# Dilated attention: keeping the queries in three token orders, copied by ScalarE one branch ahead

## The chip, the core and the metric

One core of a Trainium2 chip runs the whole program: TensorE (PE, matmuls and weight loads), VectorE (DVE), ScalarE (ACT), GpSimd (POOL) and SyncE (SP), which issues nearly all DMAs. The metric is device time of one launch, in microseconds (us); lower is better.

## The reference, cut to what matters

The layer is a bidirectional encoder block over two requests, 256 prompt tokens and 2,048 sample tokens (2,304 rows in all), with a Hyena half (long convolutions by FFT) and an attention half beside it, then an output projection and a gated MLP. The change lies in the attention half: 8 heads of 64, three dilated sliding-window branches, merged by their softmax denominators.

```
DILATED_BRANCHES = ((128, 1), (512, 4), (2048, 16))

def dilated_branch(q, k, v, slopes, window, dilation):
    ...
    R = window // (2 * dilation)          # 64 in every branch
    Ls = T // dilation
    ...
    def by_residue(a):                    # token t belongs to residue t % dilation
        return a.reshape(B, Ls, dilation, H, E).transpose(0, 2, 1, 3, 4)
    ...
    s = jnp.einsum('brnqhe,brnkhe->brnhqk', qb, kb).astype(jnp.float32) * (E ** -0.5)
    ...                                   # ALiBi bias, |rel| <= R, softmax
```

In the branch of dilation 4 a query attends to keys at distance 4, 8, ... up to 256 tokens; in that of dilation 16 to keys at 16, 32, ... tokens.

## The kernel before, in words

Queries and keys lie in DRAM head by head, transposed (`d_qT`, `d_kT`: 64 rows a head, 2,304 tokens along the free axis). `prepare` (line 851) brings one head into SBUF in four chunks of 576 tokens, each twice, on partitions 0 to 63 and 64 to 127: ScalarE rounds the queries to `Qh` (line 862), VectorE leaves the rest in `Ql` (the helper `sub`, line 201), ScalarE and GpSimd make the upper half of `Ks` the rest of the keys (line 865 and line 201), VectorE rounds the lower half (line 867). So one fp32 product is two fp32r matmuls: `Qh` and then `Ql` are the stationary operands, `Ks` streams (lines 902 and 903).

`attention` goes over four pairs of heads (hp 0 to 3), in each over three branches (b 0, 1, 2 for dilations 1, 4, 16), in each over 18 blocks of 128 queries, 216 blocks in all. For the sample, branches 0 and 1 have `win` blocks: 128 queries against a window of 192 keys at the ends of a residue and of 256 elsewhere. In branch 0 the prompt adds two such blocks; in branch 1 a residue has four blocks (192, 256, 256, 192 keys). Branch 2 has one `res` block a residue (two residues of 128 keys are streamed, 256 columns). In branches 1 and 2 the prompt is two `pack` blocks (every second token). Queries and keys both lie in natural order, so their slices step by 1, 4 or 16 tokens, by 2 in `pack` blocks:

```
t0 = off + res + dil * P * j
qs = slice(t0, t0 + dil * (P - 1) + 1, dil)
...
rhs = Ks[:, m0:m0 + dil * (n - 1) + 1:dil]
```

A block goes through these steps: four weight loads and matmuls into the scores `aS`, two of each a head (`scores`); VectorE adds the bias and takes the minimum (line 906); ScalarE takes the exponential into `aP` and its sum (line 909); `flip` transposes `aP` on TensorE into `aT` (line 918), and ScalarE, or VectorE for every third block, copies it to `aPT` (lines 922 and 925); `values` multiplies by the values into `aOp` (line 933); for every group of up to four blocks ScalarE copies `aOp` to `aOC` (line 938), TensorE transposes it (`aOT`, line 946), VectorE writes `aO` and a DMA stores it. `aS` and `aT` have two buffers each, `aOp` one. Every engine works its own instructions in order.

The Hyena half of the sample runs beside the attention, woven in by `weave` at fixed rates (90 to 440): `hs2z`, `hs2k`, `hs` matmuls, DVE products, ScalarE copies `hbe` and `hae` (lines 742 and 692). After the generators have given a program order, a scheduler sets the order on each engine from modelled durations; what is ready early moves forward.

The six tiles of a head pair (`Ql`, `Ks`, `Qh` for two heads) are allocated a head pair ahead, and `prepare` of the next pair is stepped once in six blocks (`if k % 6 == 0: next(ahead, None)`). When head pair 3 begins, the pool of the first head's tiles closes (`mq.close()`), and the pool for the start of the output projection takes its place; three weight tiles `ow` take over buffers of the tag `qk` (line 1044).

Of the kernel before, what the change touches and what calls it, by code (L numbers as in the profile page):

```python
# [13 lines left out]
F32 = mybir.dt.float32  # L14
F32R = mybir.dt.float32r
# [6 lines left out]
P = 128  # L22
D = 1024
NT = 2304
LP, LS = 256, 2048
# [162 lines left out]
class Hybrid:  # L188
# [662 lines left out]
    def prepare(self, head, tiles):  # L851

        nc = self.nc
        Ql, Ks, Qh = tiles
        up = slice(64, 128)
        hr = slice(64 * head, 64 * head + 64)
        for c0 in range(0, NT, 576):
            cc = slice(c0, c0 + 576)
            for t, src in ((Ql, self.qT), (Ks, self.kT)):
                for d in range(2):  # L860
                    nc.sync.dma_start(out=t[64 * d:64 * d + 64, cc].bitcast(F32), in_=src[hr, cc])
            nc.scalar.copy(Qh[:, cc], Ql[:, cc].bitcast(F32))
            self.sub(nc.vector, Ql[:, cc], Ql[:, cc].bitcast(F32), Qh[:, cc])
            kh = self.qkp.tile([P, 576], F32R, tag="kh", name="kh", bufs=1)
            nc.scalar.copy(kh[up], Ks[up, cc].bitcast(F32))
            self.sub(nc.gpsimd, Ks[up, cc], Ks[up, cc].bitcast(F32), kh[up])
            nc.vector.tensor_copy(Ks[0:64, cc], Ks[0:64, cc].bitcast(F32))
            yield

    def attention(self, wp, psS, psT, psO, first, mq):  # L870
        nc, a = self.nc, self.a
        q1, q2, q3 = [], [], []

        def scores(heads, g, i, blk, ot, bias, b):
            r, kind, _ = g
# [5 lines left out]
            for hh in range(2):  # L881
                Ql, Ks, Qh = heads[hh]
                t0 = off + res + dil * P * j
                qs = slice(t0, t0 + dil * (P - 1) + 1, dil)
                if kind == "win":
                    qa, qb = Qh[:, qs], Ql[:, qs]
                    k0 = max(0, P * j - 64)
                    n = min(nb * P, P * j + 192) - k0
                    v0, N = 0, n
                    b0 = k0 - (P * j - 64)  # L890
                    m0 = off + res + dil * k0
                    rhs = Ks[:, m0:m0 + dil * (n - 1) + 1:dil]
                elif kind == "res":
                    qa, qb = Qh[:, qs], Ql[:, qs]
                    e = res - res % 2
                    rhs = Ks[:, off:off + L].rearrange("p (j s) -> p s j", s=dil)[:, e:e + 2]
                    v0, n, N, b0 = P * (res % 2), P, 256, 0
                else:
                    qa, qb = Qh[:, off + j:off + L:2], Ql[:, off + j:off + L:2]
                    rhs = Ks[:, off:off + L].rearrange("p (j s) -> p s j", s=2)  # L900
                    v0, n, N, b0 = P * j, P, 256, 256 if b == 1 else 128
# [65 lines left out]

        def prepare(hp, out):

            for hh in range(2):  # L970
                if hp or hh:
                    out.append(self.qk_tiles(wp, 6) if hp % 2 else self.qk_tiles(self.ow if hh else self.qkp, 3))
            gens = [self.prepare(2 * hp + hh, out[hh]) if hp or hh else self.pre for hh in range(2)]
            for _ in range(4):
                for x in gens:
                    next(x, None)
                    yield

        k = 0
        nxt = [first]  # L980
        own = prepare(0, nxt)
        next(own)
        next(own)
        for hp in range(4):
            if hp == 3:
                mq.close()
            cs = slice(hp * P, hp * P + P)
            heads, nxt = nxt, []
            ahead = prepare(hp + 1, nxt) if hp < 3 else iter(())
            yield  # L990
            for b in range(3):
                dil = DILS[b]
                lo = (0, 256, 640)[b]
# [4 lines left out]
                for g in self.attention_groups(b, (0, 1) if hp == 3 else (1, 0)):  # L998
# [3 lines left out]
                    for i, blk in enumerate(blks):  # L1002
                        res, j, nb = blk
                        if hp == 0:
                            next(own, None)
                        sb, n = scores(heads, g, i, blk, ot, bias, b)
# [18 lines left out]
                        if len(q2) > 1:  # L1025
                            values(q2.pop(0))
            for _ in ahead:
                pass
        for y in q1:
# [22 lines left out]
    def mixers(self):  # L1052
# [48 lines left out]
        self.qkp = self.pool(mq, "m_q", side="left")  # L1101
        first = self.qk_tiles(self.qkp, 3)
        gw[0] = islice(g, 35 - gw[2])
        self.weave([h, gw], until=gw[0])
        gw[0] = g
        x = self.prepare(0, first)
        self.weave([h, gw, [x, 5, 0]], until=g)
# [587 lines left out]
```

## Time and profile before

| | |
|---|---|
| median of 3 runs | 3504.5 us (3498.43 to 3505.18) |
| the profiled execution's own time | 3498.32 us |
| its span, first to last instruction | 3496.5 us |
| granted TensorE clock, mean | 0.975 |
| PE busy in the span | 93% |
| DVE, ACT, POOL busy | 71%, 46%, 36% |
| attention, from its first scores to its last transposes | 946.7 to 1640 us |

The profiled execution lies 6.2 us below the median and beside the lowest run. The span is the profile's clock, the execution's time has some 2 us around it. "Busy" counts a matmul from its issue to its modelled end, so matmuls overlap in it; how fast TensorE goes is read from the distance between the starts of neighbouring matmuls.

### The profile page before, as it was taken

The page shows a single profiled execution, that of the slowest core. Times are in us where ns is not written, and L with a number is a line of the kernel's source. Part 1 is how long each engine was busy: PE and PEld are TensorE (multiplying, and loading weights), DVE is VectorE, ACT ScalarE, POOL GpSimd, SP SyncE. Part 2 cuts the span into 40 slices and gives each one's busy share as a digit, 9 for nine tenths or more (in the row PEclk, how much of TensorE's full clock was granted, in tenths as well). Part 3 has the DMA queues.
Part 4 walks back from the last instruction along what each step waited for, and adds up shares of the span by engine and source line. Part 5 has one row for each costly group of instructions (what it writes and reads, how often), then busy time and mean ns, then how long its engine had stood idle before and what let it go on. Part 6 is the DMA issues. An engine that isn't in the chain of part 4 may idle for free.

```text
span 3496.5 us, 57581 instructions
## 1 busy us (share of the span) xinstructions
PE 3267.9 (93%) x21142; PEld 2932.6 (84%) x21142; DVE 2492.7 (71%) x4314; ACT 1594.6 (46%) x3322; POOL 1264.4 (36%) x934
## 2 busy tenths in 40 slices
PE   6999899899889899999799899999999999899998
PEld 4987788889756676566789799999999999899998
DVE  7988878665487657685887766767766667467657
ACT  4576753323264655455455433334333334344433
POOL 1487761123231322220454433334533334123222
PEclk9999999999999999999999999999999999999999
DMA  6454457676675766658676623445444224456655
GB/s 243 133 171 130 147 181 235 217 238 200 186 223 174 211 191 197 199 188 249 185 219 182 203 96 129 147 149 198 171 157 143 86 96 148 171 191 226 210 187 176
DMA packets 407825, 628.05 MB, mean 180 GB/s; under 512 B 27919, under 2 KB 230927, under 8 KB 401623
## 3 DMA queue, kind: packets, MB, share of 16 engines
q1 hardware_dynamic: 354384, 593.13, 52.2%
q10 hardware_dynamic: 52072, 28.40, 2.8%
q8 instruction: 167, 2.74, 0.3%
q0 software_dynamic: 1088, 2.85, 0.2%
q14 instruction: 114, 0.93, 0.1%
HBM read 419.03 MB, written 205.25 MB: 179 GB/s over the span
## 4 chain that ended last, share of the span: by engine, by line
PE 40%; DVE 5%; issue 2%; DMA 2%; ACT 1%; POOL 1%; ACTq 0%; SPq 0%; DVEq 0%; POOLq 0%
PE w L208 8%; PE w L207 8%; PE w L206 8%; PE fd L208 4%; PE fd L207 4%; PE fd L206 4%; DVE fT L1260 1%; PE om L208 1%; PE om L207 1%; PE om L206 1%; DVE hl L201 0%; DMA d_x1T<-ox 0%; DMA hl<-d_opT 0%; DMA wraw<-in_w_gate 0%; DVE oO L1152 0%
## 5 line engine op out<-in xcount | busy, mean ns | idle before, releaser
L206 PE MATMUL w<-hh,whi 128*128 128x290 f32 (+1 forms) x2464 | 734.6, 299 | 16.6 <-ACT whi L1354 9.4
L208 PE MATMUL w<-hh,wlo 128*128 128x290 f32 (+1 forms) x2464 | 730.6, 298 | 11.3 <-POOL wlo L201 7.2
L207 PE MATMUL w<-hl,whi 128*128 128x288 f32 (+1 forms) x2464 | 733.8, 298 | 3.9 <-DVE hl L201 3.9
L206 PEld LDWEIGHTS w<-hh,whi 128*128 128x128 f32 x2464 | 469.1, 191 | 19.3 <-ACT whi L1354 11.0
L208 PEld LDWEIGHTS w<-hh,wlo 128*128 128x128 f32 x2464 | 468.0, 190 | 13.5 <-POOL wlo L201 8.1
L207 PEld LDWEIGHTS w<-hl,whi 128*128 128x128 f32 x2464 | 470.8, 191 | 5.5 <-DVE hl L201 5.4
L207 PE MATMUL pj<-hTlo,wihi 128*128 128x386 f32 (+1 forms) x1152 | 401.8, 349 | 7.9 <-DVE hTlo L201 7.9
L206 PE MATMUL pj<-hThi,wihi 128*128 128x386 f32 (+1 forms) x1152 | 403.1, 350 | 5.3 <-ACT u L627 3.2
L208 PE MATMUL pj<-hThi,wilo 128*128 128x386 f32 (+1 forms) x1152 | 398.9, 346 | 0.3 <-DVE wilo L201 0.3
L206 PE MATMUL fd<-hh,dwh 128*128 128x288 f32 x1210 | 360.3, 298 | 12.5 <-ACT dwh L1560 12.5
L208 PE MATMUL fd<-hh,dwl 128*128 128x288 f32 x1210 | 359.1, 297 | 0.0
L207 PE MATMUL fd<-hl,dwh 128*128 128x288 f32 x1210 | 358.0, 296 | 0.0
L733 POOL TENSOR_TENSOR ht<-ht,ht 128x512 f32<-128x512 f32 x72 | 94.6, 1314 | 445.7 <-DVE ht L732 375.8
L206 PEld LDWEIGHTS fd<-hh,dwh 128*128 128x128 f32 x1210 | 230.0, 190 | 13.2 <-ACT dwh L1560 12.7
L207 PEld LDWEIGHTS pj<-hTlo,wihi 128*128 128x128 f32 x1152 | 222.4, 193 | 20.5 <-DVE hTlo L201 9.8
L206 PEld LDWEIGHTS pj<-hThi,wihi 128*128 128x128 f32 x1152 | 221.7, 193 | 16.2 <-issue 4.0
L208 PEld LDWEIGHTS pj<-hThi,wilo 128*128 128x128 f32 x1152 | 221.8, 193 | 13.6 <-issue 8.6
L207 PEld LDWEIGHTS fd<-hl,dwh 128*128 128x128 f32 x1210 | 229.6, 190 | 0.4
L208 PEld LDWEIGHTS fd<-hh,dwl 128*128 128x128 f32 x1210 | 228.1, 189 | 0.1
L909 ACT ACTIVATE aP<-aP,aO 128x256 f32<-128x256 f32 (+2 forms) x432 | 194.1, 451 | 55.4 <-DVE aO L906 46.3
L201 POOL TENSOR_TENSOR wlo<-ws,whi 128x512 fp32r<-128x512 f32 x88 | 133.0, 1511 | 231.1 <-ACT whi L1354 231.1
L1354 ACT CAST whi<-ws 128x512 fp32r<-128x512 f32 x176 | 109.0, 620 | 230.2 <-PE w L207 186.8
(300 smaller groups left out, 7980.6 us busy)
## 6 DMA issues: line engine op xcount, KB each, us to landing
hl<-d_G SPq DMA_DIRECT2D x154, 288.0 KB, 5.2
dwl<-d_S SPq DMA_DIRECT2D x59, 704.0 KB, 4.1
wiraw<-in_w_in SPq DMA_DIRECT2D x72, 512.0 KB, 4.5
d_G<-cv SPq DMA_DIRECT2D x42, 576.0 KB, 2.9
wraw<-in_w_gate SPq DMA_DIRECT2D x22, 1024.0 KB, 4.9
wraw<-in_w_up SPq DMA_DIRECT2D x22, 1024.0 KB, 6.4
adat<-in_ada_t SPq DMA_DIRECT2D x36, 512.0 KB, 4.6
d_fA<-fae SPq DMA_DIRECT2D x72, 256.0 KB, 2.8
```

Source lines behind the costliest of these rows:

```text
L201: eng.tensor_tensor(out=lo, in0=x, in1=hi.bitcast(F32), op=ALU.subtract)
L206: mm(out, wh, xh, start=first, stop=False, skip_group_check=more)
L207: mm(out, wh, xl, start=False, stop=False, skip_group_check=more)
L208: mm(out, wl, xh, start=False, stop=last, skip_group_check=more)
L733: nc.gpsimd.tensor_tensor(out=t1, in0=t1, in1=t2, op=ALU.add)
L909: nc.scalar.activation(sb[:, hh, :n], sb[:, hh, :n], AF.Exp, scale=-1.0, bias=mn, accum_out=dn)
L1260: v.tensor_tensor(out=o, in0=x, in1=y, op=ALU.subtract)
L1354: nc.scalar.copy(hi, x)
```

## The change

The queries are no longer held in natural order through a whole head pair. `Ql` and `Qh` get tiles of their own (`q_tiles`), and there is a set for every branch: branch 0 uses natural order, branch 1 the order by residue mod 4, branch 2 by residue mod 16. While branch 0 runs, `by_residue` copies the natural tiles into the mod 4 tiles; while branch 1 runs, it copies those into the mod 16 tiles, every copy on ScalarE: for one head and one change of order eight copies of 512 tokens (four residues, `Ql` and `Qh`) and two of the prompt's 256, so 20 for the pair. The source of the first copy steps by four tokens; that of the second steps by four again, in runs of 128. The query slices of the scores then have step 1 in every branch. The keys stay in one natural tile for a head pair (`k_tile`), and their slices step as before.

`prepare` can now do queries or keys alone. Keys of the next head pair are prepared during branches 0 (first head) and 1 (second head), its natural queries during branch 2. The steps are taken once a block instead of once in six. Two sets of query tiles alternate from branch to branch. `mq.close()` moves from the start of head pair 3 to the start of its branch 2, and of the `ow` tiles two take the tag `q`, one the tag `k`.

```diff
-    def qk_tiles(self, pool, bufs):
-        return [pool.tile([P, NT], F32R, tag="qk", name=t, bufs=bufs) for t in ("Ql", "Ks", "Qh")]
+    def q_tiles(self, pool, bufs):
+        return [pool.tile([P, NT], F32R, tag="q", name=t, bufs=bufs) for t in ("Ql", "Qh")]
+
+    def k_tile(self, pool, bufs):
+        return pool.tile([P, NT], F32R, tag="k", name="Ks", bufs=bufs)
...
+    def by_residue(self, src, dst, b):
+
+        nc = self.nc
+        for res in range(4):
+            part = slice(LP + 512 * res, LP + 512 * res + 512)
+            for x, y, cp in zip(src, dst, (nc.scalar.copy, nc.scalar.copy)):
+                if b == 1:
+                    i, o = x[:, LP + res::4], y[:, part]
+                else:
+                    i = x[:, part].rearrange("p (j a) -> p a j", a=4)
+                    o = y[:, LP:].rearrange("p (a r j) -> p r a j", a=4, r=4)[:, res]
+                cp(o, i.bitcast(F32))
+                if res == 3:
+                    i, o = x[:, :LP], y[:, :LP]
+                    if b == 1:
+                        i, o = i.rearrange("p (j a) -> p a j", a=2), o.rearrange("p (a j) -> p a j", a=2)
+                    cp(o, i.bitcast(F32))
+            yield
...
-                Ql, Ks, Qh = heads[hh]
-                t0 = off + res + dil * P * j
-                qs = slice(t0, t0 + dil * (P - 1) + 1, dil)
+                (Ql, Qh), Ks = heads[hh]
+                t0 = off + P * j + (res * (L // dil) if r else 0)
+                qa, qb = Qh[:, t0:t0 + P], Ql[:, t0:t0 + P]
...
+        def queries(u, hh):
+
+            return self.q_tiles(wp, 4) if u % 2 else self.q_tiles(self.ow if hh else self.qkp, 2)
...
             for b in range(3):
+                u = 3 * hp + b
+                if u == 11:
+                    mq.close()
...
+                qs, nq = nq, [queries(u + 1, hh) for hh in range(2)] if u < 11 else []
+                heads = [(qs[hh], ks[hh]) for hh in range(2)]
+                if b < 2:
+                    gens = [self.by_residue(qs[hh], nq[hh], b + 1) for hh in range(2)]
+                    if hp < 3:
+                        nk.append(keys(hp + 1, b))
+                        gens.append(self.prepare(2 * hp + 2 + b, ks=nk[b]))
+                else:
+                    gens = [self.prepare(2 * hp + 2 + hh, nq[hh]) for hh in range(2)] if hp < 3 else []
+                ahead = chain(own, turns(gens)) if u == 0 else turns(gens)
...
-                        if k % 6 == 0:
+                        if u or k > 8:
                             next(ahead, None)
...
-            t = self.ow.tile([P, NT], F32R, tag="qk", name="ow", bufs=3)
+            t = self.ow.tile([P, NT], F32R, tag="k" if m == 2 else "q", name="ow", bufs=1 if m == 2 else 2)
```

How the engines' orders move, at three places. In these rows a line of the changed kernel stands where it is in the new file: L924 and L925 are the scores, L931 the exponentials, L940 the transposes, L944 and L947 the copies to `aPT`, L955 the values, L960 the copy to `aOC`, L968 its transposes, L867 and L871 the casts of `prepare`, L887 and L892 the copies of `by_residue`.

First, ScalarE where branch 0 of head pair 1 ends and branch 1 begins, from the exponentials of block 15 of the branch on (the two after it are the prompt's). Before:

```order
L909 ACTIVATE aP,aO<-aP,aO 128x192 x2
L922 COPY aPT<-aT 128x512
L909 ACTIVATE aP,aO<-aP,aO 128x192 x4
L925 COPY aPT<-aT 64x2x128
L925 COPY aPT<-aT 128x2x128
L909 ACTIVATE aP,aO<-aP,aO 128x192
L938 COPY aOC<-aOp 128x512
```

Changed:

```order
L931 ACTIVATE aP,aO<-aP,aO 128x192 x2
L887 CAST Ql<-Ql 128x4x128 x2
L887 CAST Qh<-Qh 128x4x128 x2
L887 CAST Ql<-Ql 128x4x128 x2
L887 CAST Qh<-Qh 128x4x128 x2
L887 CAST Ql<-Ql 128x4x128
L887 CAST Qh<-Qh 128x4x128
L887 CAST Ql<-Ql 128x4x128
L887 CAST Qh<-Qh 128x4x128
L887 CAST Ql<-Ql 128x4x128
L892 CAST Ql<-Ql 128x256
L944 COPY aPT<-aT 128x512
```

Fourteen copies (13 of 512 tokens and one of 256) now stand in one row between the exponentials of block 15 and the next copy to `aPT`; the exponentials of blocks 16 and 17 come only after it, and the last six copies a little later. Of the eight times that queries are copied, six begin like this, with 8 to 14 copies in one row (three of them with one copy to `aPT` after the first eight or ten). At the start of head pair 2 there are seven in a row and the rest are spread. At the start of head pair 0 eleven stand ahead of the first exponentials and nine more between those of blocks 3 and 4.

Second, ScalarE at the change from head pair 0 to head pair 1. Before:

```order
L742 COPY hbe<-hs_8292 128x512
L862 CAST Qh<-Ql 128x576
L922 COPY aPT<-aT 128x2x128
L909 ACTIVATE aP,aO<-aP,aO 128x128 x2
L938 COPY aOC<-aOp 128x512
L909 ACTIVATE aP,aO<-aP,aO 128x192 x2
L865 CAST kh<-Ks 64x576
```

Changed:

```order
L742 COPY hbe<-hs_8369 128x512
L887 CAST Ql<-Ql 128x512 x2
L887 CAST Qh<-Qh 128x512 x2
L887 CAST Ql<-Ql 128x512 x2
L887 CAST Qh<-Qh 128x512 x2
L944 COPY aPT<-aT 128x2x128
L887 CAST Ql<-Ql 128x512
L887 CAST Qh<-Qh 128x512
L887 CAST Ql<-Ql 128x512
L887 CAST Qh<-Qh 128x512
L887 CAST Ql<-Ql 128x512
L931 ACTIVATE aP,aO<-aP,aO 128x128
```

The casts of the next pair's queries (L862 before) have left this place; they stand in the branch of dilation 16 ahead of it. Eight copies and then five take their place, with one copy to `aPT` between.

Third, TensorE at the first of these places, after the scores of block 15. Before:

```order
L918 MATMUL aT<-ident,aP 128x128 x2
L690 MATMUL hs_8487<-hS,hf_5117 128x512
L691 MATMUL hs_8487<-hS,hf_5117 128x512
L918 MATMUL aT<-ident,aP 128x128 x2
L946 MATMUL aOT<-ident,aOC 128x128 x4
L933 MATMUL aOp<-aPT,aV 64x128 x4
L918 MATMUL aT<-ident,aP 128x128 x2
```

Changed:

```order
L940 MATMUL aT<-ident,aP 128x128 x4
L690 MATMUL hs_8597<-hS,hf_5117 128x512
L691 MATMUL hs_8597<-hS,hf_5117 128x512
L924 MATMUL aS<-Ks,Qh 128x192
L925 MATMUL aS<-Ks,Ql 128x192
L924 MATMUL aS<-Ks,Qh 128x192
L925 MATMUL aS<-Ks,Ql 128x192
L968 MATMUL aOT<-ident,aOC 128x128 x4
L955 MATMUL aOp<-aPT,aV 64x128 x4
```

After these come the scores of block 17, the four transposes of block 15, and then the values of block 14, which need the copy to `aPT` that stands behind ScalarE's fourteen. TensorE's own order has changed little here.

## Rows read from the trace of the kernel before

**Rows 1.** The page's first line.

```profile
span 3496.5 us, 57581 instructions
```

**Rows 2.** Busy time by stretch: the branches of head pairs 1 and 2, from the first scores of one to the first scores of the next. Columns: stretch, its length, then busy us (and instructions) of PE, PEld (weight loads), DVE, ACT, POOL, the granted TensorE clock, the DMA share and GB/s.

```profile
1141.50:1198.30 56.80, 47.05 (x325) 31.27 (x323) 44.78 (x126) 38.79 (x109) 22.13 (x16) 0.94 0.84 234
1198.30:1249.70 51.40, 51.38 (x335) 37.80 (x332) 27.61 (x102) 29.02 (x100) 13.25 (x10) 1.00 0.52 155
1249.70:1292.20 42.50, 42.14 (x247) 30.64 (x245) 23.29 (x104) 24.00 (x94) 12.48 (x10) 1.00 0.63 188
1292.20:1340.20 48.00, 40.22 (x320) 28.26 (x316) 38.49 (x114) 37.94 (x106) 22.07 (x15) 1.00 1.02 279
1340.20:1410.60 70.40, 69.86 (x368) 46.17 (x368) 49.85 (x140) 34.20 (x112) 11.81 (x9) 0.95 0.49 154
1410.60:1467.80 57.20, 54.39 (x252) 35.34 (x249) 38.75 (x117) 25.29 (x94) 10.22 (x8) 1.00 0.57 180
```

**Rows 3.** Timeline, a block of branch 0 (step 1), 256 keys. Columns here and in the next groups: start, duration (us), engine, line, operation.

```profile
1303.37 0.36 PE L902 MATMUL aS<-Ks,Qh 128*128 128x256 f32 x1
1303.57 0.28 PE L903 MATMUL aS<-Ks,Ql 128*128 128x256 f32 x1
1303.57 0.19 PEld L902 LDWEIGHTS aS<-Ks,Qh 128*128 128x128 f32 x1
1303.68 0.28 PE L902 MATMUL aS<-Ks,Qh 128*128 128x256 f32 x1
```

**Rows 4.** Timeline, a block of branch 1 (queries and keys step by 4), 256 keys.

```profile
1238.63 0.60 PE L902 MATMUL aS<-Ks,Qh 128*128 128x256 f32 x1
1239.05 0.42 PE L903 MATMUL aS<-Ks,Ql 128*128 128x256 f32 x1
1239.07 0.33 PEld L902 LDWEIGHTS aS<-Ks,Qh 128*128 128x128 f32 x1
1239.29 0.42 PE L902 MATMUL aS<-Ks,Qh 128*128 128x256 f32 x1
```

**Rows 5.** Timeline, a block of branch 1, 192 keys.

```profile
1220.14 0.52 PE L902 MATMUL aS<-Ks,Qh 128*128 128x192 f32 x1
1220.48 0.42 PE L903 MATMUL aS<-Ks,Ql 128*128 128x192 f32 x1
1220.71 0.42 PE L902 MATMUL aS<-Ks,Qh 128*128 128x192 f32 x1
```

**Rows 6.** Timeline, a block of branch 2 (step 16), 256 keys.

```profile
1259.79 0.57 PE L902 MATMUL aS<-Ks,Qh 128*128 128x256 f32 x1
1260.19 0.39 PE L903 MATMUL aS<-Ks,Ql 128*128 128x256 f32 x1
1260.21 0.31 PEld L902 LDWEIGHTS aS<-Ks,Qh 128*128 128x128 f32 x1
1260.40 0.39 PE L902 MATMUL aS<-Ks,Qh 128*128 128x256 f32 x1
```

**Rows 7.** Timeline, a `pack` block of the prompt (queries and keys step by 2), 256 keys, and the two Hyena matmuls after it.

```profile
1247.95 0.49 PE L902 MATMUL aS<-Ks,Qh 128*128 128x256 f32 x1
1248.26 0.41 PE L903 MATMUL aS<-Ks,Ql 128*128 128x256 f32 x1
1248.26 0.21 PEld L902 LDWEIGHTS aS<-Ks,Qh 128*128 128x128 f32 x1
1248.48 0.41 PE L902 MATMUL aS<-Ks,Qh 128*128 128x256 f32 x1
...
1248.94 0.41 PE L690 MATMUL hs<-hS,hf 128*128 128x512 f32 x1
1249.19 0.39 PE L691 MATMUL hs<-hS,hf 128*128 128x512 f32 x1
```

**Rows 8.** From the page's costliest groups: a ScalarE cast of 512 elements to fp32r, both sides in SBUF with step 1 (busy us, mean ns, then the idle time before it).

```profile
L1354 ACT CAST whi<-ws 128x512 fp32r<-128x512 f32 x176 | 109.0, 620 | 230.2 <-PE w L207 186.8
```

**Rows 9.** ScalarE's timeline at the end of branch 0 of head pair 1: a copy to `aPT` and the two exponentials of a block.

```profile
1193.15 0.59 ACT L922 COPY aPT<-aT 128x512 f32<-128x512 f32 x1 [0.24 <-PE aT L918]
1193.66 0.46 ACT L909 ACTIVATE aP<-aP,aO 128x192 f32<-128x192 f32 x1
...
1194.46 0.19 ACT L909 ACTIVATION_READ_ACCUMULATOR aP<-aP,aO 128x1 f32 x1
```

**Rows 10.** TensorE's timeline at the same place: the last scores matmul of that block, then transposes, the next block's scores (four matmuls from 1195.19), values (x8) and transposes.

```profile
1193.27 0.27 PE L903 MATMUL aS<-Ks,Ql 128*128 128x192 f32 x1
...
1194.78 0.66 PE L918 MATMUL aT<-ident,aP 128*128 128x128 f32 x4
1195.19 0.34 PE L902 MATMUL aS<-Ks,Qh 128*128 128x192 f32 x1
...
1195.79 0.66 PE L933 MATMUL aOp<-aPT,aV 128*64 128x128 f32 x8
1196.38 0.66 PE L918 MATMUL aT<-ident,aP 128*128 128x128 f32 x4
```

**Rows 11.** Groups of the attention's stretch, 946 to 1640 us (busy us, mean ns, then idle before): two parts of `prepare`, and the cast of the first output weights.

```profile
L201 DVE TENSOR_TENSOR Ql<-Ql,Qh 128x576 fp32r<-128x576 f32 x27 | 23.4, 868 | 0.1
L862 ACT CAST Qh<-Ql 128x576 fp32r<-128x576 f32 x26 | 17.4, 670 | 14.1 <-DMA Ql<-d_qT 13.8
L1190 ACT CAST ow<-oraw 128x1024 fp32r<-128x1024 f32 x3 | 3.1, 1042 | 4.4 <-DMA oraw<-in_w_out 4.4
```

More of the change, by code (lines that the diff above doesn't have):

```diff
@@ L2 @@
 from contextlib import ExitStack
-from itertools import islice
+from itertools import chain, islice
 import numpy as np
@@ L893, in scores @@
                 elif kind == "res":
-                    qa, qb = Qh[:, qs], Ql[:, qs]
                     e = res - res % 2
@@ L966, in store, with turns, keys @@
             return go
[L968 to L977, printed above, removed]
+        def turns(gens):
+            while gens:
+                for x in list(gens):
+                    if next(x, gens) is gens:
+                        gens.remove(x)
+                    else:
+                        yield
+        def queries(u, hh):
+            return self.q_tiles(wp, 4) if u % 2 else self.q_tiles(self.ow if hh else self.qkp, 2)
+        def keys(hp, hh):
+            return self.k_tile(wp, 2) if hp % 2 else self.k_tile(self.ow if hh else self.qkp, 1)
+        nq = [first[0], queries(0, 1)]
+        nk = [first[1], keys(0, 1)]
+        own = turns([self.pre, self.prepare(1, nq[1], nk[1])])
+        next(own, None)
+        next(own, None)
         k = 0
[L980 to L983, printed above, removed]
         for hp in range(4):
-            if hp == 3:
-                mq.close()
             cs = slice(hp * P, hp * P + P)
-            heads, nxt = nxt, []
-            ahead = prepare(hp + 1, nxt) if hp < 3 else iter(())
-            yield
             for b in range(3):
+                u = 3 * hp + b
+                if u == 11:
+                    mq.close()
+                if b == 0:
+                    ks, nk = nk, []
+                qs, nq = nq, [queries(u + 1, hh) for hh in range(2)] if u < 11 else []
[5 more added lines that the diff above has]
+                        gens.append(self.prepare(2 * hp + 2 + b, ks=nk[b]))
+                else:
+                    gens = [self.prepare(2 * hp + 2 + hh, nq[hh]) for hh in range(2)] if hp < 3 else []
+                ahead = chain(own, turns(gens)) if u == 0 else turns(gens)
+                yield
                 dil = DILS[b]
@@ L1003, in attention @@
                         res, j, nb = blk
-                        if hp == 0:
-                            next(own, None)
+                        if u == 0:
+                            next(ahead, None)
                         sb, n = scores(heads, g, i, blk, ot, bias, b)
@@ L1026, in attention @@
                             values(q2.pop(0))
-            for _ in ahead:
-                pass
+                for _ in ahead:
+                    pass
         for y in q1:
@@ L1101, in mixers @@
         self.qkp = self.pool(mq, "m_q", side="left")
-        first = self.qk_tiles(self.qkp, 3)
+        first = self.q_tiles(self.qkp, 2), self.k_tile(self.qkp, 1)
         gw[0] = islice(g, 35 - gw[2])
@@ L1105, in mixers @@
         gw[0] = g
-        x = self.prepare(0, first)
+        x = self.prepare(0, *first)
         self.weave([h, gw, [x, 5, 0]], until=g)
```

25 lines of the change are left out of this document (13 added, 12 removed).

## The prediction

> **What bounds the kernel now.** I read the span first [rows 1], then the busy time by branch [rows 2], then the timelines of single blocks. The attention takes 946.7 to 1640 us, a fifth of the span. [...] In branch 0 TensorE has gaps (47.05 of 56.80, 40.22 of 48.00), and VectorE and ScalarE are the busiest they get in their head pairs (38 to 45 us). [...] What decides is whether ScalarE's new work stands where TensorE waits for it.
>
> The blocks show what steps cost TensorE. With step 1 the first scores matmul is followed by the next after 0.20 us, then after 0.11; a weight load takes 0.19 [rows 3]. With step 4 and the same 256 keys it is 0.42, then 0.24, and the load takes 0.33 [rows 4]. With step 16 it is 0.40, then 0.21, the load 0.31 [rows 6]. But two things step here, the queries (loaded) and the keys (streamed), and the change takes away only the first. Two more blocks separate them. With 192 keys at step 4 the distance is still 0.23: fewer keys, the same time, so the load sets it [rows 5]. In the `pack` block, step 2, the load takes 0.21, nearly the natural 0.19, yet the matmuls still stand 0.22 apart: there the streaming keys set it [rows 7].
>
> **Part 1: natural weight loads.** A block with natural queries and stepping keys is not in the trace; the nearest row is the `pack` block, whose load is nearly natural. So I take its distances, 0.31 and then 0.22, for 256 keys. For 192 keys I scale the streaming by the keys: 0.22 x 192/256 = 0.17, an estimate from [rows 7], and about 0.25 for the first. In branch 1 a head pair has 8 blocks of 256: 0.42 - 0.31 = 0.11 on the first distance and 0.01 on each of three others, 0.14 a block, 1.1 us. Its 8 blocks of 192 save 0.34 - 0.25 = 0.09 and three times 0.06, 0.27 a block, 2.2 us. In branch 2, 16 blocks save 0.40 - 0.31 = 0.09, 1.4 us. `pack` blocks stay near where they are. Together 4.7 us a head pair, **19 us** for four. Lower end: if 192 stepping keys cost as much as 256, those blocks save only 0.34 - 0.31 = 0.03 each, which leaves 11. An upper end of all distances falling to those of step 1 [rows 3] is excluded by the `pack` block [rows 7]; I keep 22, for the matmuls behind a block. All of it is in branches where TensorE is full, so I count it whole.
>
> **Part 2: the copies on ScalarE.** 16 of 512 tokens and 4 of 256 for each of eight changes of order. A cast of 512 with step 1 takes 620 ns [rows 8]; one behind another an instruction of this length occupies ScalarE for 0.51 (1193.15 to 1193.66 [rows 9]), one of 256 for about 0.3 (estimate, half and the fixed part). 16 x 0.51 + 4 x 0.3 = 9.4 us a change, 75 us in all. No ScalarE instruction of this trace steps through SBUF. Below, a step costs nothing, 0.51; above, it doubles the time, as it nearly doubles TensorE's load and stream, 1.0. I take 0.51, since the stepping stream of the `pack` block [rows 7] still brings a column in 0.22/256 us, 0.86 ns, and ScalarE's element takes no less (0.51/512 us, 1.0 ns): the slower reading is still fast enough for it.
>
> 75 us would fit into ScalarE's room if they were spread. By the order they are not: 8 to 14 stand in one row, ahead of exponentials that TensorE needs. Take the place of the first and third order listings. ScalarE finishes a block's exponentials 1.2 us after its last scores matmul (1193.27 to 1194.46 [rows 9, 10]). Then 13 x 0.51 + 0.3 = 6.9 us of copies, then 0.6 for the copy to `aPT` that the next values need: 8.7 us after those scores. TensorE has until then two sets of transposes (0.41 each, 1194.78 to 1195.19), two blocks of natural scores (0.60 each, 1195.19 to 1195.79), four transposes of `aOT` (0.41, as the others), four values matmuls (0.59 for eight, so 0.3 [rows 10]) and the pair L690 and L691 (0.25 each, 1248.94 to 1249.19 [rows 7]): 3.2 us. It waits 5.5 us. Two score buffers and two of `aT` allow no more lead. Where one copy to `aPT` stands after eight copies, the first wait is about half of that and a second follows. I take 4.5 us for each of six such places, 27, and 1 for the broken row at head pair 2: **+28 us**. Ends: 0, if TensorE's lead is larger than I read, and 44 with eight times 5.5. The eleven copies ahead of the first exponentials and the nine at block 3 of head pair 0 cost **+4** more (0 to 8).
>
> **Part 3: `prepare` moves.** Its instructions and DMAs are the same in number (eight chunks of queries and of keys a head pair, SP issues two DMAs a chunk and operand). The query half leaves branch 0 of a pair for branch 2 of the same: 8 x 0.87 on VectorE, 8 x 0.67 on ScalarE [rows 11]. Branch 0 is relieved where VectorE is fullest; branch 2 has room (23.29 of 42.50 and 38.75 of 57.20 us of VectorE [rows 2]). I count **-4 us** for three pairs (-10 to 0). The DMAs are issued early in branch 2 and have 40 us to land. The three `ow` weights (cast 1.04 us each [rows 11]) now wait for branch 2 of head pair 3, since their tiles free only then; their cover is the rest of that branch, some 45 us; if it fell short, the first output matmuls would wait. I count 0.
>
> **Part 4: the clock.** [...]
>
> **Sum.** -19 + 28 + 4 - 4 + 5 = +14 on the profiled execution's 3498.3. That execution lies 6 us under the median of the runs, 3504.5; the change is counted from the median, and rounded up for ScalarE's fuller branch 0: **3520 us**, +0.4%. A measurement of this kernel can tell about 0.2%, 7 us.
>
> **Rivals.**
>
> *The copies fit in (faster).* ScalarE was idle for half of the branches, and the order may be less tight on the chip than I read it. Then part 1 and part 3 stay: -23, and some 3 of waits, 3484. It decides at waits of about 2 us a place: 19 + 4 = 4 + 5 + 7 x 2. For it speaks ScalarE's mean load [rows 2]; against it the row of fourteen. 0.20.
>
> *Gain and waits cancel.* Waits near 2 us: 3504, between 3497.5 and 3511.5. 0.19.
>
> *The keys bound it all.* If stepping keys hold every distance where it is, 192 keys included, part 1 falls to 0 and the copies stay: 3504.5 + 33 = 3538. For it, two blocks [rows 4, 7]: 0.24 against 0.22 for 256 keys with quite different loads. Against it, the first distance, 0.42 against 0.31. 0.12.
>
> *Stepping reads double the copies.* Each takes 1.0: a row of fourteen lasts 6.4 us longer, seven places, +45: 3565. For it, TensorE's doubling; against it, the 0.86 ns above. [...] 0.08.
>
> *The change does not do what it says.* The order shows natural slices at the scores and all copies on ScalarE, so nothing is left for this.
>
> **How the numbers follow.** The forecast has 0.41, the keys' rival 0.12, the doubled copies 0.08: slower by over 0.2%, 0.61. Within 0.2%, 0.19; faster, 0.20. The range goes from just above the faster rival's 3484, half of which it leaves out, to 3548: 3520 and most of the upper ends of parts 2 and 4, with the keys' rival inside and the doubled copies outside. The slower cases' own range is 3512 to 3565.
>
> **What would show it.** Weight loads of the scores at 0.19 in all branches; distances between scores matmuls of 0.17 at 192 keys and still near 0.22 at 256. `Ql` and `Qh` copies of 0.6 us in rows of 8 to 14 at the branches' starts, and TensorE idle for 3 to 5 us there, waiting for ScalarE's exponentials and copies. I am wrong if these waits stay under 2 us, if 256 stepping keys fall well under 0.2, or if the copies last 1 us.

## The result and the profile after

| | kernel before | changed kernel |
|---|---|---|
| median, us | 3503.95 (4 runs) | 3547.93 (4 runs) |
| profiled execution, us | 3498.3 | 3545.1 |
| span, us | 3496.5 | 3543.3 |
| mean granted clock | 0.975 | 0.964 |
| first to end of last scores, us | 946.8 to 1635.3 | 943.8 to 1688.5 |
| end of the last Hyena matmul, us | 1658.7 | 1665.4 |
| end of the output projection's matmuls, us | 1925.1 | 1975.2 |

The ratio is 1.0127, 95% interval 1.0108 to 1.0145: slower by 44 us, where 3520 was forecast. The sign was right; the size is nearly three times the +16 that was forecast, at the very top of the range. Of the later runs, two executions fell far out of line (4,401 us in `e9`, 7,775 us in `e10`), and all times and ratios below leave them out. The span grew by 46.8, and the attention by 56 (688.5 to 744.7). After the last scores 3 us less pass until the output projection is done (289.8 before, 286.6 now); no Hyena matmul is left over by then.

The two pages' first lines stand against each other [rows 1]:

```profile
span 3543.3 us, 57757 instructions
```

The natural loads came as forecast. Below is TensorE's timeline of the changed kernel in branch 1 of head pair 1: a block of 256 keys, then one of 192, against [rows 4, 5].

```profile
1246.40 0.48 PE L924 MATMUL aS<-Ks,Qh 128*128 128x256 f32 x1
1246.69 0.41 PE L925 MATMUL aS<-Ks,Ql 128*128 128x256 f32 x1
1246.93 0.41 PE L924 MATMUL aS<-Ks,Qh 128*128 128x256 f32 x1
...
1249.15 0.42 PE L924 MATMUL aS<-Ks,Qh 128*128 128x192 f32 x1
1249.39 0.35 PE L925 MATMUL aS<-Ks,Ql 128*128 128x192 f32 x1
1249.57 0.36 PE L924 MATMUL aS<-Ks,Qh 128*128 128x192 f32 x1
1249.57 0.21 PEld L925 LDWEIGHTS aS<-Ks,Ql 128*128 128x128 f32 x1
```

Read the starts. With 256 keys the distances are 0.29 and 0.24 (0.42 and 0.24 before; 0.31 and 0.22 taken), with 192 keys 0.24 and 0.18 (0.34 and 0.23 before; 0.25 and 0.17 taken). The weight loads take 0.19 to 0.21, where they took 0.33.

The copies did not come as forecast. From the groups of ScalarE in the attention, by shape (busy us, mean ns of one, idle before), against the cast with step 1 [rows 8]:

```profile
L887 ACT CAST Qh<-Qh 128x512 fp32r<-128x512 f32 x64 | 70.2, 1118 | 0.0
L887 ACT CAST Ql<-Ql 128x512 fp32r<-128x512 f32 x64 | 70.0, 1115 | 4.6 <-PE aS L924 4.5
L892 ACT CAST Ql<-Ql 128x256 fp32r<-128x256 f32 x16 | 6.8, 425 | 0.0
L892 ACT CAST Qh<-Qh 128x256 fp32r<-128x256 f32 x16 | 6.8, 423 | 0.0
```

A copy of 512 takes 1.12 us where 0.62 was assumed, and occupies ScalarE for about 1.0. In all the copies hold ScalarE for 142 us (their durations, which overlap, add up to 154), not for the 75 of the forecast. The place where branch 1 of head pair 1 begins shows the cost: first ScalarE, then TensorE (the last column in brackets is idle time and what ended it). [Rows 9, 10] show the end of branch 0 there in the kernel before.

```profile
1214.20 2.16 ACT L887 CAST Ql<-Ql 128x512 fp32r<-128x512 f32 x2 [0.33 <-PE aS L924]
1216.27 2.21 ACT L887 CAST Qh<-Qh 128x512 fp32r<-128x512 f32 x2
...
1226.42 1.09 ACT L887 CAST Ql<-Ql 128x512 fp32r<-128x512 f32 x1
1227.41 0.40 ACT L892 CAST Ql<-Ql 128x256 fp32r<-128x256 f32 x1
1227.72 0.58 ACT L944 COPY aPT<-aT 128x512 f32<-128x512 f32 x1
```

```profile
1211.25 0.28 PE L925 MATMUL aS<-Ks,Ql 128*128 128x192 f32 x1
...
1218.94 1.08 PE L776 MATMUL hs<-hD,hgi 128*64 128x512 f32 x4
1220.90 0.47 PE L690 MATMUL hs<-hS,hf 128*128 128x512 f32 x1 [0.88 <-DVE hg L777]
1221.21 0.40 PE L691 MATMUL hs<-hS,hf 128*128 128x512 f32 x1
1228.35 2.17 PE L955 MATMUL aOp<-aPT,aV 128*64 128x128 f32 x16 [6.75 <-ACT aPT L944]
```

Fourteen copies hold ScalarE for 13.5 us, from 1214.20 to 1227.7. TensorE has work until 1221.6, 7.4 us from the row's start, and then stands for 6.75 until the copy to `aPT` behind the row. Two readings follow. The row is twice as long as forecast. And TensorE's lead, the work that it still has when the row begins, is longer than I read: counted as in the prediction, from the last scores matmul of the block ahead of the row (1211.25), it keeps going for 10.4 us, not for 3.2. The longest row, at the same change in head pair 2, has 18 copies, 16 us from 1384.59 on, and TensorE waits 5.73 us behind it.

The whole attention's waits say the same (TensorE; waited-for engine and line; us in total, times, longest), first the changed kernel, then the kernel before:

```profile
PE aT L940 <- ACT aP L931: 20.3, 9, 5.7
PE aOp L955 <- ACT aPT L944: 17.8, 6, 6.7
```

```profile
PE aT L918 <- ACT aP L909: 4.4, 3, 2.3
PE aOp L933 <- ACT aPT L922: 3.3, 4, 2.0
```

Summed over all lines of that view, TensorE waits for ScalarE for 51.9 us, before for 10.6: 41 more. The granted clock fell as well. Branch 0 of head pair 1, the first row of [rows 2], is now:

```profile
1152.90:1216.10 63.20, 46.84 (x325) 32.16 (x322) 32.78 (x113) 52.88 (x124) 22.34 (x16) 0.81 0.62 183
```

TensorE's busy time is as before (46.84 against 47.05), ScalarE's rose from 38.79 to 52.88, VectorE's fell from 44.78 to 32.78 as the query half of `prepare` left the branch, and the granted clock went from 0.94 to 0.81. By windows of 2 us it is 0.50 or 0.98 to 1.00 nearly everywhere; 11 of the stretch's windows show 0.50 here, one in the kernel before, and three in each lie between. Since TensorE's busy time there did not grow, this stretch alone does not show that the fall cost time. From the first to the last scores it is different (before, then changed; columns as in [rows 2]):

```profile
946.80:1635.30 688.50, 650.14 (x3696) 430.71 (x3695) 488.26 (x1450) 380.28 (x1223) 170.75 (x122) 0.98 0.68 203
943.80:1688.50 744.70, 655.29 (x3716) 408.64 (x3714) 501.29 (x1471) 514.94 (x1383) 173.05 (x126) 0.93 0.64 192
```

TensorE idles for 89 us, 51 more than before, and is busy for 5 us more although the natural loads shorten its work.

### The profile page after: what moved, and what is told of

Same layout as the page of the kernel before. It is cut to its first block, busy times and chain, and to the rows that moved or that the text cites. A ratio compares the mean times of both kernels' runs of the same rounds, so it can differ in the third digit from the quotient of the medians.

```text
span 3543.3 us, 57757 instructions
## 1 busy us (share of the span) xinstructions
PE 3269.6 (92%) x21142; PEld 2913.9 (82%) x21142; DVE 2489.2 (70%) x4314; ACT 1726.9 (49%) x3482; POOL 1263.5 (36%) x934
## 4 chain that ended last, share of the span: by engine, by line
PE 42%; DVE 5%; issue 2%; DMA 1%; ACT 1%; POOL 1%; ACTq 0%; SPq 0%; DVEq 0%; POOLq 0%
PE w L208 9%; PE w L206 9%; PE w L207 9%; PE fd L208 4%; PE fd L207 4%; PE fd L206 4%; DVE fT L1298 0%; POOL oat L1192 0%; DVE ohy L1206 0%; PE om L206 0%; DVE hl L201 0%; DMA oO<-d_O 0%; PE om L207 0%; PE om L208 0%; DVE ox L1261 0%
## 5 line engine op out<-in xcount | busy, mean ns | idle before, releaser
L206 PE MATMUL w<-hh,whi 128*128 128x288 f32 (+1 forms) x2464 | 736.8, 300 | 12.7 <-ACT whi L1392 8.4
L931 ACT ACTIVATE aP<-aP,aO 128x256 f32<-128x256 f32 (+2 forms) x432 | 194.0, 452 | 46.5 <-DVE aO L928 29.0
```

Of the source, the lines that this page charges most:

```text
L206: mm(out, wh, xh, start=first, stop=False, skip_group_check=more)
L931: nc.scalar.activation(sb[:, hh, :n], sb[:, hh, :n], AF.Exp, scale=-1.0, bias=mn, accum_out=dn)
```

## The experiments

Three theories stand in the first expectations. **L**: what costs is the length of the copies in a row ahead of exponentials. **S**: ScalarE's total load. **O**: something else in the change (the moved preparation, the later output weights, the clock). The ratios below are to the kernel before on the same chip, where its median was 3495.2 for the first four runs, 3496.1 for the next four and 3493.0 for `e9` to `e11`. `e8` and `e12` ran once each and have no ratio. The difference of two ratios is good to 5 to 8 us by their intervals. The expectations of `e1` to `e4` count from the first result, where the kernel before had 3504; against a number of theirs a measured time is set by its distance from the kernel before.

**One size of the copies: their reading step (`e1`).**

```diff
-                    i, o = x[:, LP + res::4], y[:, part]
+                    i, o = x[:, part], y[:, part]
```

(and likewise for branch 2 and the prompt)

> The changed kernel with copies that read step 1: the same number of copies, the same destinations and nearly the same places, but the queries in the branches of dilations 4 and 16 are then the wrong tokens. Theories. L (length in a row): the copies take 1.1 us because they read with a step of 16 bytes, and 8 to 14 of them in a row keep back the exponentials; with step 1 they take 0.62 and the forecast's own sum returns: 3520 us (3512 to 3528). S (sum): what counts is ScalarE's total load, wherever the copies stand; its added load halves, 3525. O (other): the 44 us come from what else moved (keys and queries prepared elsewhere, output weights later, clock): 3540 or more.

Measured: 3505.0, ratio 1.0029 [1.0018, 1.0040]. The copies are back at the ordinary cast's time:

```profile
L887 ACT CAST Qh<-Qh 128x512 fp32r<-128x512 f32 x64 | 37.9, 615 | 0.0
L887 ACT CAST Ql<-Ql 128x512 fp32r<-128x512 f32 x64 | 37.9, 616 | 3.7 <-PE aS L924 3.6
```

Against this run the change costs 0.0098, 34 of the 44 us. TensorE's waits for ScalarE are 12.1 us here, hardly over the 10.6 of the kernel before, but they stand elsewhere: 8.1 of them right behind rows of five or more copies. Three rows here have 14 or 15 copies and last 7.0 to 7.7 us; behind two TensorE does not wait for ScalarE, behind the third it does:

```profile
1156.45 2.05 PE L739 MATMUL hs<-ht,htab 128*128 128x512 f32 x2 [3.65 <-ACT hbe L742]
```

The run is 10 us over the kernel before, where L had +16 (+8 to +24), S +21 and O +36 or more. One reservation: the scheduler placed the work anew, so TensorE's order agrees with that of the changed kernel in 18,341 of 21,142 positions only, and the rows are cut differently (at the place above 10 copies, not 14). The run with the step on the writing side, below, has no such difference.

**The same copies, spread (`e2`).** Each copy is queued behind the exponentials of the block at which it is taken.

```diff
-                cp(o, i.bitcast(F32))
+                with self.tc.issue_after(self.exp.ins):
+                    cp(o, i.bitcast(F32))
...
```

> The changed kernel, the copies unchanged in number, step and length, but each step of two to four copies is queued on ScalarE behind the exponentials of the block at which the program takes it, so that no row of more than four stands there. L: the waits of 4 to 7 us at the changes of branch go; 3490 to 3508. S: ScalarE's load is as before, 3535 to 3550. O: 3540 or more.

Measured: 3502.2, ratio 1.0015 [1.0004, 1.0027], with copies of 1.12 us as in the change. ScalarE's load is the same and 39 us are gone, so S falls (it had +31; L had -14 to +4, and +5 came out). TensorE's waits for ScalarE are 27.3 us, the longest 3.0 where the change had 6.7:

```profile
PE aT L942 <- ACT aP L933: 9.1, 9, 3.0
PE aOp L957 <- ACT aPT L946: 7.6, 13, 1.6
```

**No copies, with natural (`e3`) and with stepping loads (`e4`).** In both, the preparation stays where the change put it.

```diff
-                    gens = [self.by_residue(qs[hh], nq[hh], b + 1) for hh in range(2)]
+                    gens = []
...
```

> The changed kernel without any copy: the natural tile serves all three branches, read with step 1, so that the branches of dilations 4 and 16 use the wrong queries. It shows what natural weight loads and the moved preparation are worth with no copies: parts 1 and 3 of the forecast, -19 and -4: 3481 us (3475 to 3491) by L and S. By O it stays above 3520.

The second also restores the slices of the kernel before:

```diff
-                qa, qb = Qh[:, t0:t0 + P], Ql[:, t0:t0 + P]
+                qs = slice(t0, t0 + st * (P - 1) + 1, st)
+                qa, qb = Qh[:, qs], Ql[:, qs]
...
```

> The changed kernel without copies and with the query slices stepping through the natural tile as before: what stays of the change is the new places of the preparation of keys and queries, the smaller tiles and the later start of the output weights. L and S: part 3 of the forecast alone, -4: 3500 us (3494 to 3506). O: above 3520. The difference to the kernel without copies is the worth of natural weight loads alone, forecast at 19 us.

Measured: 3507.9, ratio 1.0034 [1.0022, 1.0047], and 3523.4, ratio 1.0078 [1.0063, 1.0093]. They were to be 23 and 4 us faster than the kernel before, and are 12 and 27 slower. TensorE, VectorE, ScalarE and GpSimd have the same order in both, so their difference is the loads, 16 us. But what `e4` keeps of the change, with no copies and no natural loads, costs 27 us: the preparation at its new places and in finer steps, the smaller tiles, the later output weights. That is what theory O had for this run (over 3520), though not for `e3`. No run takes these parts singly. The place is behind the attention. These are the Hyena matmuls left after the last scores (count, busy us, mean ns, idle before), in the kernel before and in `e4`:

```profile
L776 PE MATMUL hs<-hD,hgi 128*64 128x512 f32 x20 | 7.3, 812 | 7.7 <-issue 6.6 <-DVE hg L777 1.1
```

```profile
L776 PE MATMUL hs<-hD,hgi 128*64 128x512 f32 x44 | 17.2, 872 | 15.2 <-DVE hg L777 15.2
```

44 are left, not 20, in eleven groups of four among the first output rows, and before six of the groups TensorE waits for VectorE. The last scores end 10 us earlier (1625.3), but from the last scores to the end of the output projection 324 us pass, not 290. In every kernel with Hyena matmuls left over, the projection ends 266 to 268 us after the last of them; in the others, 286 to 291 us after the last scores.

**Copies of half the length (`e5`)**, in number and place as before.

```diff
-                    i, o = x[:, LP + res::4], y[:, part]
+                    i, o = x[:, part][:, :256], y[:, part][:, :256]
...
```

> The copies are as in the changed kernel in number, place and row, but each is of 256 tokens (128 for the short ones) and reads with step 1; the scores of branches 1 and 2 read those halves twice, so their tokens are wrong. A copy should take about 0.42 us, one behind another about 0.30, against 0.55 in the plain copies and 1.0 in the change. Theory L (what a row costs is what it lasts beyond TensorE's lead of about 3 us): a row of thirteen lasts 3.9 us, so the waits at the rows nearly vanish; 3490 to 3498 us where the kernel before has 3495, some 10 less than the plain copies. Theory P (each copy costs in proportion to its time, wherever the lead stands; 34 us for 0.45 us more from the plain copies to the change): 17 less than the plain copies, 3488. Theory O (the moved preparation and the later output weights cost some 10 us whatever the copies do): 3505, as the plain copies.

Measured: 3493.5, ratio 0.9999 [0.9990, 1.0009]; a copy takes 0.40 us. TensorE's waits for ScalarE are 5.1 us. The time is 10 less than that of the plain copies, as L had it (P had 17, O none). But those 10 are more than the 7 us of ScalarE waits that went; the order of the work differs again (18,253 of TensorE's 21,142 positions as in the plain copies), so a few us stay unassigned.

**The step on the writing side (`e6`).**

```diff
-                    i, o = x[:, LP + res::4], y[:, part]
+                    i = x[:, part].rearrange("p (j a) -> p j a", a=4)
+                    o = y[:, LP:].rearrange("p (a r j) -> p r j a", a=4, r=4)[:, res]
...
```

> The copies read 512 neighbouring tokens with step 1 and write them with a step (2048 bytes in branch 1, 512 or 2048 in branch 2), in the same rows; the tiles end up the same as in the change. Theory R (only a stepping read is slow): copies of 0.62 us, 0.55 one behind another, and the time of the plain copies, 3505 where the kernel before has 3495. Theory W (a step on either side makes ScalarE as slow): copies of 1.1 us and the time of the change, ratio 1.012, 3538. Theory W+ (a stepping write costs more than a stepping read): copies above 1.2 us, over 3550.

Measured: 3537.3, ratio 1.0118 [1.0101, 1.0135]: theory W. The copies of 512 write 2048 bytes apart in both branches; 512 bytes apart write only the prompt's in branch 1. Writing with that step, 1.10 us, is as slow as reading with one of 16 bytes, 1.12:

```profile
L888 ACT CAST Qh<-Qh 128x512 fp32r<-128x512 f32 x64 | 67.1, 1096 | 0.0
```

This run and the plain copies have the same instructions in the same order on TensorE, VectorE, ScalarE and GpSimd, so here nothing differs but the writing step of the copies, and with it their length: 0.0089, 31 us. TensorE's waits for ScalarE rise from 12.1 to 46.5 us. The attention as a whole, plain copies and then this run:

```profile
946.30:1651.40 705.10, 642.10 (x3719) 402.77 (x3718) 495.85 (x1471) 454.44 (x1389) 175.03 (x126) 0.96 0.67 203
950.20:1685.30 735.10, 658.30 (x3720) 410.61 (x3719) 497.20 (x1471) 504.45 (x1389) 174.97 (x126) 0.93 0.64 194
```

It is 30 us longer, and TensorE's idle time grows by only 14 of them (63.0 to 76.8), since other waits shrink as those for ScalarE grow. The other 16 are the same matmuls taking longer (642.1 to 658.3) while the granted clock falls from 0.96 to 0.93. So about half of what the long copies cost comes through the clock; that is a reading of these two lines, and no run holds the clock fixed.

The same, spread (`e7`):

> As the spread copies (each step of the copying queued behind the exponentials of its block), but reading with step 1 and writing with a step. By theory R the copies take half the time as well: ScalarE's load falls by 35 us, and 3492 to 3500 us where the kernel before has 3495 and the spread copies had 3502. By theory W: the same as the spread copies, 3502.

Measured: 3493.1, ratio 0.9994 [0.9984, 1.0005], the fastest of the versions that leave nothing of the layer out, and no different from the kernel before. The copies take 1.10 us, so theory R, which gave this time, has the wrong reason. Theory W had the time of the spread copies, 7 us more by the ratios. What took the 7 us off is not shown: TensorE's waits for ScalarE are 17.6 us against 27.3, and its order agrees in 20,494 of 21,142 positions.

**Other steps of reading (`e8`)**, 8 bytes for branch 1 and 12 for branch 2.

```diff
-                    i, o = x[:, LP + res::4], y[:, part]
+                    i, o = x[:, LP + res:LP + res + 1023:2], y[:, part]
-                    i = x[:, part].rearrange("p (j a) -> p a j", a=4)
+                    i = x[:, res:res + 1534:3].rearrange("p (a j) -> p a j", a=4)
```

> The copies of 512 read with a step of 8 bytes (those for branch 1) and of 12 bytes (those for branch 2) in place of 16; wrong tokens. It shows how a copy's time depends on the step. [...] Rival (any step doubles the time): 1.11 at both. Time: between the plain copies and the change by the first, 3505 to 3525; as the change by the second, 3538.

Measured: 3521.8, inside the 3505 to 3525 expected for a time between the plain copies and the change; the rival's 1.11 us at both steps does not appear. The groups of ScalarE in branch 0 of head pair 0 (step 8 bytes), then in branch 1 (12 bytes):

```profile
L887 ACT CAST Ql<-Ql 128x512 fp32r<-128x512 f32 x8 | 5.3, 658 | 0.0
```

```profile
L887 ACT CAST Ql<-Ql 128x512 fp32r<-128x512 f32 x4 | 3.5, 891 | 0.0
```

So 0.62, 0.66, 0.89 and 1.12 us at 4, 8, 12 and 16 bytes: nearly free up to 8, then, less some 0.2 us of fixed time (an estimate from 0.40 and 0.62 us at 256 and 512 elements), in proportion to the step.

**Natural loads in the kernel before (`e9`, `e12`)**, nothing copied or moved.

```diff
-                t0 = off + res + dil * P * j
-                qs = slice(t0, t0 + dil * (P - 1) + 1, dil)
+                t0 = off + P * j + (res * (L // dil) if r else 0)
+                qs = slice(t0, t0 + P)
...
```

> The kernel before, with one edit: the scores load the same queries from neighbouring tokens, in step 1 (wrong tokens in branches 1 and 2). No copies, nothing moved, the order on TensorE the same as before. Theory T (the output stage ends by whichever is later, 287 us after the last scores or 267 us after the last Hyena matmul, and in the kernel before both are at their limit): the attention gets 18 to 20 us shorter, the Hyena matmuls that stand among it move up with it, and those left behind it wait for VectorE, so that a part of the gain is lost: 3478 to 3490 where the kernel before has 3495. Rival N (the natural loads are worth 19 us wherever they stand, and the plain preparation cost the rest): 3476. Rival M (Hyena ends the stage alone): 3493 to 3497.

Measured: 3477.2, ratio 0.9958 [0.9946, 0.9971], 16 us less: M falls, and T's upper end and N lie too near to each other for the time to part them. The same kernel was run once more for a profile that can:

> The kernel before with natural query loads once more, for a profile at the usual clock, since the one of the first run was taken at a clock of 0.65. It is to show where its 16 us came from, against the run without copies, which has the same loads and 12 us more than the kernel before. If the 16 us lie in the scores of branches 1 and 2: last scores some 16 to 20 us earlier than before, the last Hyena matmul earlier by as much, and the output stage 287 to 291 us behind the last scores as in the kernel before. If the rest of Hyena took a part: the output stage over 295 us behind the last scores.

Measured: 3478.6. The last scores end at 1615.5 (1635.3 before), the last Hyena matmul at 1637.2 (1658.7), the output projection at 1905.2 (1925.1): all three 20 us earlier, 289.7 us from the first to the third. In the order of the kernel before, which is kept on TensorE to the last matmul, the gain lands whole, as N had it; the loss that T expected, in waits for VectorE, does not appear. The run without copies has the same loads, and its last scores even end at 1605.5, but its last Hyena matmul at 1662.2. There the gain lands as well, against `e4`, which has the same order (1625.3 and 1682.0); what both pay is the longer Hyena rest.

**Natural keys as well (`e10`)**, added to that.

```diff
-                    rhs = Ks[:, m0:m0 + dil * (n - 1) + 1:dil]
+                    m0 = min(off + res * 128 * (dil > 1) + k0, NT - n)
+                    rhs = Ks[:, m0:m0 + n]
...
```

> As the run before, and the keys too are read with step 1 (wrong tokens). It removes both halves of what a step costs TensorE in the scores. The distance between scores matmuls of 256 keys should fall from 0.22 to 0.12 and of 192 keys to 0.11. By these the attention has 16 blocks of 256 with 0.42 to 0.20 and three of 0.24 to 0.12, and 8 of 192, in a head pair: some 0.5 us a block, 60 to 70 us of TensorE in all beyond the kernel before. Theory T: the last scores come 50 us or more earlier, the last Hyena matmul far less, and the output stage ends 267 us after that: 3465 to 3485. Rival N: 3430.

Measured: 3439.1, ratio 0.9847 [0.9828, 0.9866], below what T had: the last Hyena matmul ends at 1594.7, 64 us earlier than in the kernel before, and the last scores at 1570.4, 65 us earlier. It moves with the attention as long as the order is the same, so T's fixed Hyena end falls. The distances at 256 keys in branch 1:

```profile
1182.41 0.37 PE L903 MATMUL aS<-Ks,Qh 128*128 128x256 f32 x1
1182.61 0.28 PE L904 MATMUL aS<-Ks,Ql 128*128 128x256 f32 x1
1182.73 0.28 PE L903 MATMUL aS<-Ks,Qh 128*128 128x256 f32 x1
1182.85 0.28 PE L904 MATMUL aS<-Ks,Ql 128*128 128x256 f32 x1
```

0.20 and then 0.12, where stepping keys had 0.24 with stepping [rows 4] and with natural loads alike: the stepping keys set it. They cost 38 us, more than twice what the stepping queries do.

**Plain copies with stepping loads (`e11`)**, the slices as in `e4`.

> The plain copies (natural order copied with step 1, the same rows), with the scores loading from them by the steps of the kernel before. It has the order on TensorE of the plain copies, with no Hyena matmul behind the last scores, and differs from that run in the steps of the loads alone. Theory T (here the attention alone ends the stage): 17 to 21 us slower than the plain copies, 3522 to 3526 where the kernel before has 3495. Rival M: within 5 us of the plain copies, 3505 to 3510.

Measured: 3520.0, ratio 1.0086 [1.0069, 1.0103], 0.0057 or 20 us over the plain copies, with the same order on the four engines: the loads again. It holds all of the change but the natural loads and the doubled copies (the tokens of branch 2 are wrong), and costs 30 us. TensorE waits 11.3 us for ScalarE in it, as in the kernel before. More is waited for elsewhere: 10.8 us in four waits for Hyena's `hx` (0.4 in the kernel before), and 11.2 us for VectorE's minimum (5.9 before):

```profile
PE aS L926 <- DVE aO L930: 11.2, 12, 2.1
PE hs2z L725 <- DMA hx<-d_hA: 10.8, 4, 3.6
```

And all Hyena matmuls stand within the attention, 20 more than before, first in the kernel before and then in this run:

```profile
L776 PE MATMUL hs<-hD,hgi 128*64 128x512 f32 x108 | 28.8, 612 | 2.0 <-DMA hD<-d_hB 1.2 <-DVE hg L777 0.5 <-DVE aO L906 0.2
L776 PE MATMUL hs<-hD,hgi 128*64 128x512 f32 x128 | 34.2, 612 | 1.4 <-DVE hg L777 1.0 <-DMA hD<-d_hB 0.4
```

That is 5 us of work, against 3 saved behind the attention.

**The three theories.** S has fallen. L holds for the length of the copies, 31 us at the same order and 34 of the change's 44. O holds for the rest: without the long copies and the natural loads the change still costs 30 us.

## Why the prediction was right or wrong

- **Natural loads, -19: right.** Measured alone 16 us (`e9`), by difference 16 (`e3`, `e4`) and 20 (`e1`, `e11`), in all three pairs at the same order. The distances at 192 and 256 keys came within 0.02 us of those taken.
- **The copies' length, 0.51 us: wrong, and the step that failed.** It was taken at the lower bound because TensorE's stepping stream still brought a column in 0.86 ns. That row was no measure for ScalarE's reads, by its engine and by its step: it steps by 8 bytes, where ScalarE's copy too is nearly as fast as without a step (0.66 us, `e8`), and the copies step by 16. There they take 1.8 ns an element (an estimate: 0.92 us for 512, from 1.12 less the fixed 0.2) and hold ScalarE for 1.0 us each. That copies of 1 us would prove it wrong, the prediction had said. The rival *stepping reads double the copies*, given 0.08, had copies of 1.0 us and 45 us more for them; the doubling cost 34.
- **The waits of +28 at copies of 0.51: wrong.** At that length (`e1`) 8 us of waits stand behind rows, and in all TensorE waits for ScalarE 12.1 us in the attention, 10.6 before. I had counted 3.2 us of work from a block's last scores matmul to the values that wait; at the place above it was 10.4, with the first blocks of the next branch and two groups of Hyena matmuls in it. A row of thirteen at 0.51 and one of 0.3 lasts 6.9 us and would be nearly hidden there, where TensorE's work ends 7.4 us after the row's start. At 1.0 it lasts 13.5, and waits of the size that was forecast appear, 41 us more in all.
- **`prepare` moves, -4: wrong.** What `e4` keeps of the change costs 27 us. VectorE was relieved in branch 0 as said, but the order in which TensorE works through Hyena changed with the move, and I had priced only the moved instructions. What of it stays in the changed kernel is not separated: without the loads' gain and the doubling, the rest of the change costs 30 us (`e11`), in Hyena's waits and its matmuls drawn into the attention, and in the single-length copies, of which half the length took 10 us off (`e5`, at another order).
- **The clock, +5: not shown as a term.** No run shows what waits of that length cost through the clock; the +5, and the 10 above it in the range, were the author's estimate. What the runs showed: the mean fell from 0.975 to 0.964. With the long copies alone (`e1` to `e6`) TensorE's busy time in the attention grew by 16 us as the granted clock there fell from 0.96 to 0.93. That the clock is the reason is read from these figures and not tried by itself.
- **The sum.** Forecast +14: -19 for the loads, +33 for the rest at single-length copies. Measured: -20 and +30, which is +10 (`e1`), and then +34 for the doubling. That the forecast for single-length copies was nearly right in size is luck, since two of its terms were wrong in opposite directions: 8 us of waits at the rows and not 32, and a cost of the moved work instead of a gain. Nor does it speak for the mechanism that the measured 3547.93 still lies inside the range to 3548: the range left doubled copies out, and with them the prediction's own sum was 3565.

The moved preparation changes the order; *why* so much more of Hyena is left over then was not tried apart from it.

## What to carry to other kernels

Before ScalarE is given a re-ordering copy, take its time for the byte step it has, read or written, from a row with that step: a row of another engine at another step did not stand in for it here (TensorE brought a column in 0.86 ns at 8 bytes, ScalarE took 1.8 ns an element at 16, the estimate above). Then compare the length of a row of such copies with the consumer's lead at that place, counted from the order over every queued instruction; longer rows are worth spreading, a few copies behind each block's exponentials, which here gave back 39 of 44 us at the same load. And where two streams share an engine, a gain in one landed here whole in every pair of kernels with the same order (16, 16 and 20 us); where an edit changes the order, look at how much of the second stream is left when the first is done, and do not compare two kernels by one term before their orders have been compared.

## What the runs showed of the hardware that was not expected

- ScalarE, 512 fp32 elements from SBUF to SBUF: 0.62, 0.66, 0.89 and 1.12 us with reads 4, 8, 12 and 16 bytes apart, and 1.10 with contiguous reads and writes 2048 bytes apart (`e6`).
- TensorE differs: its stream already takes twice as long at 8 bytes (0.22 us for 256 columns [rows 7], 0.12 natural in `e10`), and hardly more at 16 (0.24 [rows 4]).
- Longer copies on ScalarE, at the same order on the four engines, went with 14 us more of idle time on TensorE and with 16 us more of busy time for the same matmuls, at a granted clock of 0.93 in place of 0.96 (`e1`, `e6`).
